# Early-input order in the first microseconds, and stage passages without GpSimd's weight parts

## The chip, the cores and the metric
One core of a Trainium2 chip runs the whole program in one launch. The time is the device time of an execution in microseconds. On this core TensorE (PE) multiplies, VectorE (DVE), ScalarE (ACT) and GpSimd (POOL) do the element-wise work, and SyncE (SP) and ScalarE issue the DMA transfers.

## The reference
Two transformer-like blocks over 256 latent tokens of width 1024, in float32. The first has two layers; in each, 256 context tokens `hc` go along with the latent `h`, and both are modulated by a vector worked out from `c`:

```python
m = (silu(c) @ w_ada + b_ada)                      # 9 x 1024 per layer
h  = post(h,  swiglu(pre(h,  m, 0, 0),  ffn_wi[0], ffn_wo[0]), m, 0, 1, 0.5)
hc = post(hc, swiglu(pre(hc, mc, 0, 0), ffn_wi[0], ffn_wo[0]), mc, 0, 1, 0.5)
...                                                # attention of context and latent, w_o
h = post(h, swiglu(pre(h, m, 6, 4), ffn_wi[1], ffn_wo[1]), m, 6, 5, 0.5)
```

`pre` is an RMS norm with gain and shift, `post` adds the normed and gated result to the residual. The last layer ends with the latent alone. The second block runs over the 256 tokens: a mixer of two scans, a feed-forward product with a short convolution, a gated linear attention, a second feed-forward product; each is `x + norm(f(norm(x)))`.

## The kernel before
**Weights.** All weight matrices are one stream of 128x128 tiles in the order of use, eight to a block of 512 KB. `Weights._dma` loads a block into `raw` (three buffers) by SyncE's queue. `Weights._split` makes two parts of it, `hi`, the block rounded to the matmul's reduced float format (ScalarE, L115), and `lo = raw - hi` (VectorE, L116). A product is then three matmuls, hi by hi, hi by lo, lo by hi (`mm3`, `mm3t`). Where `aside` is above zero, the low part is GpSimd's (L116 on POOL); where `alone` holds too, GpSimd makes the high part as well, as an addition of zero (L113). In the first mixer (`share = 3`) every third low part is GpSimd's. `place` says in which buffers a block's parts go, if not in the three standing pairs. `take` hands out tiles and splits two blocks ahead (`LOOK`), unless the stream is `held`; `to(b)` splits up to block b at once, and `go_on` releases the hold.

**Order.** A scheduler puts each engine's instructions in order by priority and the code's order; each engine then runs its list strictly in that order. `high_priority` moves instructions forward in the list.

**The head.** `run` issues the loads of the vectors (`vec`), the inputs (`hl`, `hc`) and constants on ScalarE's queue; `ada_loads` issues on SyncE's queue the modulation weights of eight chunks (`adaw`, four transfers of 256 KB per chunk), with the first weight blocks between. `pre` squares and norms the four row tiles (`rms_rows`, `hn`), transposes chunk by chunk (`tr`), scales by the modulation (`ux`, ScalarE) and splits the result into `uh` and `ul` (VectorE). `ada_pe` works the modulation of chunk c out: matmuls `adp`, copy `adsb`, transposes `adt`, a reduction, `mod`, `Am`. `group` runs the first products `gp` over the eight chunks with five accumulators (`NG0`).

**The passages.** The program is: feed-forward, attention, feed-forward, feed-forward (512 columns, latent and context together), attention, feed-forward (256 columns), mixer, feed-forward, mixer, feed-forward. A 256-column stage ends with `out_main` and `out_tail`: the product `po` of the last matrix, 16 last products for two row tiles; then per tile a square on ScalarE, `bi`, `yg` and `y` (times the gain), the reciprocal `rs`, the residual `hl` in two halves, the square `jv` on VectorE, and `hn` for the next stage's transposes. The next stage's first blocks are split here too, so that its first products find them. In the 512-column stages `go_on(2)` gives two low parts to GpSimd; `aj` is VectorE's modulation work of later layers.

## Time and profile before

| | us |
|---|---|
| median of 3 runs | 2624.83 (2623.13 to 2625.05) |
| the profiled execution, its own time | 2620.6 |
| its span | 2618.7 |
| TensorE busy | 2532.6 |
| VectorE busy | 1748.1 |
| ScalarE busy | 1156.1 |
| GpSimd busy | 203.9 |

The span is the profiled execution from its first to its last instruction. A busy TensorE is one that has a matmul under way, at whatever clock was granted. The profile names instructions by line, engine, and the tiles written and read (`out<-in`); a number in square brackets behind an instruction is the engine's idle time ahead of it, and what ended that.

### The profile page before, as it was taken

The numbers are of one execution on the slowest core, as the hardware profiler recorded it, in microseconds if no ns is written. First come the engines' busy times: TensorE is split into PE (matmuls) and PEld (weight loads), VectorE is DVE, ScalarE is ACT, GpSimd is POOL, SyncE is SP. The second block draws the span as 40 slices with busy tenths as digits, with TensorE's granted clock in tenths as the row PEclk, the third lists the DMA queues.
The fourth block names the chain that finished last, engine by engine and source line by source line (L and its number), as shares of the span: only waits on it lengthen the run. The fifth ranks groups of instructions, "written<-read, shape, count | busy, mean of one in ns | idle before, by whom it ended". The sixth has DMA issues, their size and how long they took to land.

```text
span 2618.7 us, 37016 instructions
## 1 busy us (share of the span) xinstructions
PE 2532.6 (97%) x13876; PEld 2137.4 (82%) x13876; DVE 1748.1 (67%) x3538; ACT 1156.1 (44%) x1994; POOL 203.9 (8%) x129
## 2 busy tenths in 40 slices
PE   6999999999999999999999999999999899999998
PEld 3888888888888887888888887987977799776997
DVE  4899535565899324998325666557767787666884
ACT  2322224455422223322224555446556565565663
POOL 2000000000000000000000101002352200121000
PEclk9999999999999999999999999999999999999999
DMA  6566331212366222565222313554433355534454
GB/s 254 182 219 216 123 120 63 82 53 73 134 220 214 92 97 97 178 220 189 97 89 87 111 69 136 184 189 150 150 125 128 120 178 186 171 111 137 153 182 157
DMA packets 124741, 375.53 MB, mean 143 GB/s; under 512 B 13840, under 2 KB 15504, under 8 KB 124304
## 3 DMA queue, kind: packets, MB, share of 16 engines
q1 hardware_dynamic: 123408, 369.22, 41.1%
q10 hardware_dynamic: 1152, 3.94, 0.4%
q8 instruction: 109, 1.79, 0.3%
q14 instruction: 72, 0.59, 0.1%
HBM read 372.05 MB, written 1.05 MB: 142 GB/s over the span
## 4 chain that ended last, share of the span: by engine, by line
PE 88%; DVE 6%; ACT 3%; issue 1%; DMA 1%; POOL 1%; SPq 0%; DVEq 0%; ACTq 0%; POOLq 0%
PE pj L172 15%; PE pj L173 15%; PE pj L174 15%; PE po L179 8%; PE po L181 8%; PE po L180 8%; PE pv L708 2%; PE tm L180 1%; PE tm L179 1%; PE tm L181 1%; DVE w L116 1%; PE gp L173 1%; PE gp L172 1%; PE gp L174 1%; ACT w L115 1%
## 5 line engine op out<-in xcount | busy, mean ns | idle before, releaser
L115 ACT ACTIVATE w<-raw 128x1024 fp32r<-128x1024 f32 (+1 forms) x564 | 572.5, 1022 | 984.5 <-PE pj L173 341.4
L116 DVE TENSOR_TENSOR w<-raw,w 128x1024 fp32r<-128x1024 f32 (+1 forms) x533 | 627.5, 1184 | 476.5 <-ACT w L115 468.8
L172 PE MATMUL pj<-uh,w 128*128 128x256 f32 (+1 forms) x2376 | 798.5, 336 | 2.4 <-ACT P L190 2.4
L174 PE MATMUL pj<-uh,w 128*128 128x256 f32 (+1 forms) x2376 | 795.0, 335 | 0.0
L173 PE MATMUL pj<-ul,w 128*128 128x256 f32 (+1 forms) x2376 | 794.6, 334 | 0.0
L172 PEld LDWEIGHTS pj<-uh,w 128*128 128x128 f32 x2376 | 451.9, 190 | 51.6 <-ACT P L190 2.8
L174 PEld LDWEIGHTS pj<-uh,w 128*128 128x128 f32 x2376 | 452.0, 190 | 48.5 <-issue 0.3
L173 PEld LDWEIGHTS pj<-ul,w 128*128 128x128 f32 x2376 | 452.1, 190 | 47.1
L597 DVE SCALAR_TENSOR_TENSOR aj<-adaw,cB 128x512 f32<-128x512 f32 x512 | 360.4, 704 | 9.0 <-DMA adaw<-in_wada 0.2
L179 PE MATMUL po<-w,sh 128*128 128x512 f32 x792 | 312.7, 395 | 0.0
L181 PE MATMUL po<-w,sl 128*128 128x512 f32 x792 | 311.9, 394 | 0.0
L180 PE MATMUL po<-w,sh 128*128 128x512 f32 x792 | 311.2, 393 | 0.0
L181 PEld LDWEIGHTS po<-w,sl 128*128 128x128 f32 x792 | 149.0, 188 | 33.9
L179 PEld LDWEIGHTS po<-w,sh 128*128 128x128 f32 x792 | 148.9, 188 | 33.8 <-DVE yg L193 0.6
L180 PEld LDWEIGHTS po<-w,sh 128*128 128x128 f32 x792 | 148.9, 188 | 33.2 <-DVE w L116 0.3
L116 POOL TENSOR_TENSOR w<-raw,w 128x1024 fp32r<-128x1024 f32 (+1 forms) x46 | 111.7, 2428 | 799.8 <-ACT w L115 784.3
L179 PE MATMUL tm<-w,uh 128*128 128x512 f32 x224 | 90.7, 407 | 0.0
L180 PE MATMUL tm<-w,uh 128*128 128x512 f32 x224 | 88.9, 397 | 0.7 <-POOL w L116 0.5
L193 DVE TENSOR_TENSOR sg<-sg,pj 128x512 f32<-128x512 f32 (+1 forms) x82 | 50.8, 619 | 58.0 <-PE pj L174 57.7
L181 PE MATMUL tm<-w,ul 128*128 128x512 f32 x224 | 88.7, 396 | 0.0
L190 ACT ACTIVATE ux<-tr,mod,Am 128x256 f32<-128x256 f32 (+1 forms) x96 | 49.8, 545 | 71.0 <-PE tr L327 26.4
L327 PE MATMUL tr<-cst,hn 128*128 128x128 f32 x240 | 51.5, 298 | 27.9 <-DVE hn L203 25.7
(340 smaller groups left out, 3139.6 us busy)
## 6 DMA issues: line engine op xcount, KB each, us to landing
raw<-in_w SPq DMA_DIRECT2D x554, 512.0 KB, 3.3
adaw<-in_wada SPq DMA_DIRECT2D x288, 256.0 KB, 3.1
bt<-in_bias SPq DMA_DIRECT2D x12, 192.0 KB, 2.4
hl<-in_x ACTq DMA_DIRECT2D x1, 1024.0 KB, 8.6
hc<-in_x ACTq DMA_DIRECT2D x1, 1024.0 KB, 8.4
gc<-in_gcst ACTq DMA_DIRECT2D x1, 512.0 KB, 3.4
out<-hl SPq DMA_DIRECT2D x2, 256.0 KB, 2.2
out<-hl ACTq DMA_DIRECT2D x2, 256.0 KB, 2.3
```

The lines of the kernel that those rows point to most:

```text
L115: nc.scalar.activation(out=hi, in_=ri, func=ACTF.Copy)
L116: eng.tensor_tensor(out=lo, in0=ri, in1=hi.bitcast(F32), op=ALU.subtract)
L172: mm(ps, w[0], x[0], start=first, stop=False)
L173: mm(ps, w[0], x[1], start=False, stop=False)
L174: mm(ps, w[1], x[0], start=False, stop=last)
L179: mm(ps, x[0], w[0], start=first, stop=False)
L180: mm(ps, x[0], w[1], start=False, stop=False)
L181: mm(ps, x[1], w[0], start=False, stop=last)
L193: self.nc.vector.tensor_tensor(out=out, in0=a, in1=b, op=op)
L327: nc.tensor.transpose(p[:, t * 128:(t + 1) * 128], hn[t][c // 4][:, (c % 4) * 128:(c % 4 + 1) * 128], self.ident)
L597: nc.vector.scalar_tensor_tensor(out=x, in0=w, scalar=1.0, in1=self.cB[:, s, i * 512:(i + 1) * 512], op0=ALU.mult, op1=ALU.mult, accum_out ...
L708: nc.tensor.matmul(po[:, a * 64:a * 64 + 64], x[:, kt * 128:(kt + 1) * 128], vt[k0 + kt][:, vc + a * 64:vc + a * 64 + 64], start=kt == 0, ...
```

## The change
1. In the head, `vec`, the second half of `hl` and the second half of `hc` are issued on SyncE's queue, the first halves on ScalarE's. Two one-element activations load ScalarE's tables for Silu and for the square root ahead of their first use. The first three blocks' parts are no longer GpSimd's. `after_norms` ties the parts of the first five blocks, by order edges within an engine's list, behind the last square and the last `hn`, then behind the `ux` and `ul` of chunks; `ada_pe` of chunk c is tied behind the products `gp` of chunk c-2.
2. In the passages, GpSimd makes no parts: `aside` is no longer set, and `go_on(2)` is `go_on(0)`. The 23 low parts that `share` gives it in the first mixer stay. All others go to ScalarE and VectorE.
3. `out_main` splits up to six blocks ahead and one past the product's end, in place of four and the end. The list of extra places is used twice in a product of more than 16 blocks (feed-forward), so that the parts can be made that early. A place is set for the block three past the end.
4. The pool `up` waits by tile (`reuse_waits="tile"`): a new tile there waits for the users of its own bytes alone.

The products on TensorE are the same, in number and shape. GpSimd loses 21 whole and 2 half low parts and its 15 high parts; ScalarE gets 9 whole and 10 half high parts and two one-element activations more, VectorE 17 whole and 10 half low parts. The rest of the difference is that halves and wholes change places. The diff, cut to what matters:

```diff
             while self.dma_at <= b:
                 self._dma()
             r = self.raws.pop(b)
-            with self.B.tc.high_priority() if urgent and b >= self.B.EARLY else nullcontext():
+            with self.B.tc.high_priority() if urgent and b >= self.B.EARLY else self.B.after_norms():
                 aside = self.aside > 0
                 eng = nc.gpsimd if aside or self.share and b % self.share == 0 else nc.vector
                 self.aside = max(0, self.aside - 1)
...
         self.nc.vector.reciprocal(t, t)
         return t
 
+    @contextmanager
+    def after_norms(self):
+
+        with ExitStack() as es:
+            for x in self.behind[(0, 2, 3, 4, 6)[self.W.split_at]] if self.W.split_at < self.EARLY else ():
+                es.enter_context(self.tc.issue_after(x.ins))
+            yield
+
     def preload(self, func, dep):
 
...
         else:
-            self.sq(h[:, 512:1024], ss[1])
+            self.behind[0][0] = self.sq(h[:, 512:1024], ss[1])
         return self.rstd(ss[1], 1024.0, [128, 1], bias=b)
 
     def normed(self, pool, t):
...
                     for i in range(2):
-                        self.ts(hn[t][i], h[:, i * 512:(i + 1) * 512], r, None, ALU.mult)
+                        self.behind[0][1] = self.ts(hn[t][i], h[:, i * 512:(i + 1) * 512], r, None, ALU.mult)
             for c in range(8):
-                if c == 2 and T == 512:
-                    self.W.go_on(2)
+                if T == 512 and (c == 2 if self.W.pos > NG0 * 8 else c == 7):
+                    self.W.go_on(0)
                 if need is not None:
                     need(c)
                 if c not in us:
...
                         else:
-                            self.act(x[:, o], p[:, o], ACTF.Identity, scale=A(c, t // 2), bias=shift(c, t // 2))
+                            g = self.act(x[:, o], p[:, o], ACTF.Identity, scale=A(c, t // 2), bias=shift(c, t // 2))
                     o = slice(t0 * 128, (t0 + by) * 128)
                     if shift is not None:
                         self.cp(us[c][0][:, o], x[:, o])
-                        self.tt(us[c][1][:, o], x[:, o], us[c][0][:, o].bitcast(F32), ALU.subtract)
+                        v = self.tt(us[c][1][:, o], x[:, o], us[c][0][:, o].bitcast(F32), ALU.subtract)
+                        self.behind.append([g, v])
                 yield us[c], o
 
     def pre1(self, pool, l, k, T, by=None, need=None):
...
 
+
         end = self.W.pos // TPB + n
-        self.W.place.update(zip(range(end - len(places), end), places))
+        m = len(places)
+        self.W.place.update(zip(range(end - m, end), places))
+        if n > 16:
+            self.W.place.update(zip(range(end - 2 * m - 3, end - m - 3), places))
+        if self.up is not None:
+            self.W.place[end + 3] = self.fourth()
         for k in range(n - 4):
             for i in range(2):
                 w = self.W.take(4)
                 if i == 0 and not self.W.held:
-                    self.W.to(min(self.W.pos // TPB + self.LOOK + 2, end))
+                    self.W.to(min(self.W.pos // TPB + 6, end + 1))
                 for t in range(2):
                     if (t, i) not in po:
                         po[t, i] = self.psum("po")
@@ -438,16 +453,10 @@
 
         yg, ss = {}, {}
         g = self.gain_rows([lambda c, i=i: G(i * 4 + c, 0) for i in range(2)])
-        self.W.held = self.W.alone = True
+        self.W.held = True
         ws = [[self.W.take(4) for i in range(2)] for _ in range(4)]
         b = self.W.pos // TPB + 3
-        self.W.to(b - 1)
-        self.W.aside = 1
-        self.W.to(b)
-        if self.up is not None:
-            self.W.place[b] = self.fourth()
-            self.W.aside = 1
-            self.W.to(b + 1)
+        self.W.to(b + 1 if b in self.W.place else b)
         for t in range(2):
             if before is not None:
                 before(t)
...
             c = m % 8
             if m == 8:
-                self.W.go_on(2)
+                self.W.go_on(0)
             if m < 8:
                 if halves:
                     self.W.held = True
                 u.append(x)
                 ws.append([self.W.take() for _ in range(n)])
-            for p, w in zip(ps, ws[c]):
-                self.mm3(p[:, o], w, (x[0][:, o], x[1][:, o]), c == 0, c == 7)
+            for i, (p, w) in enumerate(zip(ps, ws[c])):
+                g = self.mm3(p[:, o], w, (x[0][:, o], x[1][:, o]), c == 0, c == 7)
+                if self.ada_at < 8 and (m == 0 and i == 0 or i == n - 1):
+                    self.ada_behind.append(g)
         return ps, u
 
     def group256(self, us, place):
 
         b = self.W.pos // TPB
-        self.W.held = self.W.alone = True
+        self.W.held = True
         if self.W.split_at <= b + 3:
...
             m = self.mod[l][:, j:j + dj + 1:dj, :]
             two = lambda name, i, d: self.v(name, i, d + 1)[:, ::d].unsqueeze(2).to_broadcast([128, 2, 2])
             if self.ada_at < 8:
-                with self.tc.high_priority() if self.ada_at not in (1, 2) else nullcontext():
+                g = self.ada_behind[self.ada_at - 1:self.ada_at] if self.ada_at else ()
+                with ExitStack() as es:
+                    es.enter_context(self.tc.high_priority())
+                    for x in g:
+                        es.enter_context(self.tc.issue_after(x.ins))
                     self.ada_pe(m)
             else:
                 self.ada_dve(m)
...
             self.vec = const.tile([128, NVEC], F32, name="vec")
             self.cst = const.tile([128, NCST], F32, name="cst")
-            nc.scalar.dma_start(out=self.vec, in_=A["vec"])
-            nc.scalar.dma_start(out=self.hl, in_=A["x"][:, 0:2])
+            nc.sync.dma_start(out=self.vec, in_=A["vec"])
+            nc.scalar.dma_start(out=self.hl[:, 0], in_=A["x"][:, 0])
             nc.scalar.dma_start(out=self.cst, in_=A["cst"])
+            nc.sync.dma_start(out=self.hl[:, 1], in_=A["x"][:, 1])
             self.ident = self.cst[:, 0:128]
             self.blk = self.cst[:, 128:130]
             self.eps = const.tile([128, 1], F32, name="eps")
             nc.vector.memset(self.eps, 1e-6)
+            self.preload(ACTF.Silu, self.eps)
             self.zero = const.tile([128, 1], F32, name="zero")
             nc.vector.memset(self.zero, 0.0)
             self.av = const.tile([128, 32], F32, name="av")
...
                 b1 = e1.enter_context(tc.tile_pool(name="b1", bufs=1))
                 self.hc = b1.tile([128, 2, 1024], F32, name="hc")
-                nc.scalar.dma_start(out=self.hc, in_=A["x"][:, 2:4])
+                nc.scalar.dma_start(out=self.hc[:, 0], in_=A["x"][:, 2])
+                nc.sync.dma_start(out=self.hc[:, 1], in_=A["x"][:, 3])
...
                 self.act(self.cT[:, :, 0:2], cv, ACTF.Silu)
+                self.preload(ACTF.Sqrt, self.cT[:, 0, 0:1])
                 self.cB = b1.tile([128, 2, 1024], F32, name="cB")
                 self.ac = b1.tile([128, NACST], F32, name="ac")
                 self.ada_at = 0
+                self.ada_behind = []
                 self.p1 = e1.enter_context(tc.tile_pool(name="p1", bufs=54))
                 self.adp = e1.enter_context(tc.tile_pool(name="adp", bufs=1))
                 self.ada_loads()
-                self.W.aside, self.W.alone = 2, True
                 self.ffn1(0, 0, 512, 32, NG0, lambda c: self.ada_to(c + 1), (0, 1))
                 self.attn(0, False, 0, (0, 2))
                 self.ffn1(0, 1, 512, 52, nxt=(1, 0))
                 self.ffn1(1, 0, 512, 72, nxt=(1, 1))
                 self.attn(1, True, 72)
                 self.ffn1(1, 1, 256, 72, 4)
-            self.up = ent(name="up", bufs=16)
+            self.up = ent(name="up", bufs=16, reuse_waits="tile")
             self.W.share = 3
             self.by_act = True
             self.mixer0()
```

On ScalarE at the head, between the squares of `hc` and the scaled chunks (`jk` is a square, `rs` the root, `ux` the scaled chunk, `w` a high part of a block), before:

```order
L190 ACTIVATE jk,ss<-hc 128x512 x2
L190 ACTIVATE rs<-ss,bi 128x1
L190 ACTIVATE jk,ss<-hc 128x512 x2
L190 ACTIVATE rs<-ss,bi 128x1
L190 ACTIVATE ux<-tr,mod_91,Am_93 128x256 x12
L115 ACTIVATE w<-raw 128x1024
L190 ACTIVATE ux<-tr,mod_91,Am_93 128x256 x4
```
and now:

```order
L191 ACTIVATE jk,ss<-hc 128x512 x2
L191 ACTIVATE rs<-ss,bi 128x1
L191 ACTIVATE jk,ss<-hc 128x512 x2
L115 ACTIVATE w<-raw 128x1024
L191 ACTIVATE rs<-ss,bi 128x1
L191 ACTIVATE ux<-tr,mod_95,Am_97 128x256 x4
L115 ACTIVATE w<-raw 128x1024
L191 ACTIVATE ux<-tr,mod_95,Am_97 128x256 x2
```
The first block's high part stands ahead of the last tile's root, and the next ones between the chunks.

On VectorE at the end of the attention of the second layer, ahead of the 256-column feed-forward product (`w` is a low part, `G` the gain, `bi` to `hl` the first row tile's residual), before:

```order
L116 TENSOR_TENSOR w<-raw,w 128x512 x6
L208 COPY G<-gr 128x512
L116 TENSOR_TENSOR w<-raw,w 128x512 x2
L116 TENSOR_TENSOR w<-raw,w 128x1024
L205 TENSOR_SCALAR bi<-ss 128x1
L193 TENSOR_TENSOR yg<-po,G 128x512
L116 TENSOR_TENSOR w<-raw,w 128x1024
L193 TENSOR_TENSOR y_13898<-po,G 128x512
L241 RECIPROCAL rs<-rs 128x1
L199 SCALAR_TENSOR_TENSOR hl<-yg,rs,hl 128x512
```
and now:

```order
L116 TENSOR_TENSOR w<-raw,w 128x512 x6
L209 COPY G<-gr 128x512
L116 TENSOR_TENSOR w<-raw,w 128x512 x2
L116 TENSOR_TENSOR w<-raw,w 128x1024 x3
L116 TENSOR_TENSOR w<-raw,w 128x512 x2
L206 TENSOR_SCALAR bi<-ss 128x1
L194 TENSOR_TENSOR yg<-po,G 128x512
L194 TENSOR_TENSOR y_13914<-po,G 128x512
L242 RECIPROCAL rs<-rs 128x1
L200 SCALAR_TENSOR_TENSOR hl<-yg,rs,hl 128x512
```
The whole low part that stood behind `yg` has moved ahead of `bi`, and one more whole and two halves with it.

On VectorE at the end of the second mixer, ahead of the last feed-forward product (`oo` and `mxl` are the mixer's output and its low part), before:

```order
L199 SCALAR_TENSOR_TENSOR oo<-oo,rs,sr 128x256 x4
L116 TENSOR_TENSOR w<-raw,w 128x1024 x2
L199 SCALAR_TENSOR_TENSOR mxl<-tf,vec,mxh 128x256 x3
L116 TENSOR_TENSOR w<-raw,w 128x1024 x2
L199 SCALAR_TENSOR_TENSOR mxl<-tf,vec,mxh 128x256
L205 TENSOR_SCALAR bi<-ss 128x1
L193 TENSOR_TENSOR yg<-po,G 128x512
L193 TENSOR_TENSOR y_22450<-po,G 128x512
L241 RECIPROCAL rs<-rs 128x1
L199 SCALAR_TENSOR_TENSOR hl<-yg,rs,hl 128x512
```
and now:

```order
L200 SCALAR_TENSOR_TENSOR oo<-oo,rs,sr 128x256 x4
L116 TENSOR_TENSOR w<-raw,w 128x1024 x2
L200 SCALAR_TENSOR_TENSOR mxl<-tf,vec,mxh 128x256 x3
L116 TENSOR_TENSOR w<-raw,w 128x1024 x2
L200 SCALAR_TENSOR_TENSOR mxl<-tf,vec,mxh 128x256
L116 TENSOR_TENSOR w<-raw,w 128x1024
L206 TENSOR_SCALAR bi<-ss 128x1
L194 TENSOR_TENSOR yg<-po,G 128x512
L116 TENSOR_TENSOR w<-raw,w 128x1024
L194 TENSOR_TENSOR y_22472<-po,G 128x512
L242 RECIPROCAL rs<-rs 128x1
L200 SCALAR_TENSOR_TENSOR hl<-yg,rs,hl 128x512
```
Two more low parts: one ahead of `bi`, one between `yg` and `y`.

## Rows read from the trace of the kernel before

**Rows 1.** Page, part 1, TensorE to GpSimd: busy time, share, instructions.
```profile
PE 2532.6 (97%) x13876; PEld 2137.4 (82%) x13876; DVE 1748.1 (67%) x3538; ACT 1156.1 (44%) x1994; POOL 203.9 (8%) x129
```

**Rows 2.** Waits of TensorE: engine, line waited for; us in all, times, longest.
```profile
PE tr L327 <- DVE hn L203: 25.7, 11, 4.7
```

**Rows 3.** Timeline, TensorE, head: start, duration, instruction; first weight matmul.
```profile
33.46 0.49 PE L172 MATMUL gp<-uh,w 128*128 128x512 f32 x1
```

**Rows 4.** Windows: length, busy times, clock (PEclk), DMA share, GB/s; head, two passages.
```profile
24.00:33.46 9.46, 3.94 (x24) 2.11 (x24) 6.81 (x15) 3.63 (x10) 4.15 (x2) 0.52 1.04 397
1794.30:1801.20 6.90, 4.49 (x12) 3.41 (x13) 5.69 (x11) 3.61 (x14) 4.64 (x4) 0.51 0.13 39
2268.80:2275.60 6.80, 4.21 (x12) 3.00 (x13) 6.76 (x13) 2.79 (x9) 4.09 (x2) 0.50 0.45 153
```

**Rows 5.** Timeline, GpSimd, head: first and last of six.
```profile
15.03 1.94 POOL L113 TENSOR_TENSOR w<-raw,zero 128x1024 fp32r<-128x1024 f32 x1 [14.58 <-DMA raw<-in_w]
...
25.83 2.40 POOL L116 TENSOR_TENSOR w<-raw,w 128x1024 fp32r<-128x1024 f32 x1
```

**Rows 6.** Timeline, VectorE, head: two `hn` pairs beside GpSimd, one after.
```profile
19.51 4.49 DVE L203 TENSOR_SCALAR hn<-hl,rs 128x512 f32<-128x512 f32 x2
...
24.68 3.83 DVE L203 TENSOR_SCALAR hn<-hc,rs 128x512 f32<-128x512 f32 x2
...
29.20 0.88 DVE L203 TENSOR_SCALAR hn<-hc,rs 128x512 f32<-128x512 f32 x2
```

**Rows 7.** Timeline, TensorE, passages: first instruction after each long wait.
```profile
684.88 0.71 PE L172 MATMUL gp<-uh,w 128*128 128x256 f32 x2 [1.72 <-DVE uh L208]
...
1064.28 0.50 PE L172 MATMUL gp<-uh,w 128*128 128x256 f32 x2 [1.65 <-DVE uh L208]
...
1596.77 1.82 PE L327 MATMUL tr<-cst,hn 128*128 128x128 f32 x5 [4.73 <-DVE hn L203]
...
1796.71 0.80 PE L179 MATMUL gp<-w,uh 128*128 128x512 f32 x1 [2.76 <-ACT uh L190]
...
2070.02 0.50 PE L181 MATMUL po<-w,mxl 128*128 128x512 f32 x1 [2.94 <-DVE bi L205]
...
2270.81 0.90 PE L327 MATMUL tr<-cst,hn 128*128 128x128 f32 x3 [4.24 <-DVE hn L203]
...
2419.51 0.87 PE L327 MATMUL tr<-cst,hn 128*128 128x128 f32 x3 [3.63 <-DVE hn L203]
```

**Rows 8.** Timeline, VectorE, passages: beside GpSimd and alone.
```profile
681.88 2.73 DVE L597 SCALAR_TENSOR_TENSOR aj<-adaw,cB 128x512 f32<-128x512 f32 x1
...
685.87 0.68 DVE L597 SCALAR_TENSOR_TENSOR aj<-adaw,cB 128x512 f32<-128x512 f32 x1
...
1590.91 2.86 DVE L199 SCALAR_TENSOR_TENSOR hl<-y,rs,hl 128x512 f32<-128x512 f32 x1
...
1795.51 0.75 DVE L199 SCALAR_TENSOR_TENSOR hl<-yg,rs,hl 128x512 f32<-128x512 f32 x1
...
2269.56 3.70 DVE L203 TENSOR_SCALAR hn<-hl,rs 128x512 f32<-128x512 f32 x2
```

**Rows 9.** Page, part 5: parts of a block, busy us, mean ns | idle, releaser.
```profile
L115 ACT ACTIVATE w<-raw 128x1024 fp32r<-128x1024 f32 (+1 forms) x564 | 572.5, 1022 | 984.5 <-PE pj L173 341.4
L116 DVE TENSOR_TENSOR w<-raw,w 128x1024 fp32r<-128x1024 f32 (+1 forms) x533 | 627.5, 1184 | 476.5 <-ACT w L115 468.8
```

**Rows 10.** Timeline, ScalarE, head: first square, root's table, first scaled chunk.
```profile
9.85 0.63 ACT L190 ACTIVATE jk<-hl 128x512 f32<-128x512 f32 x1 [2.17 <-DMA hl<-in_x]
...
11.34 1.28 ACT L190 ACT_TABLE_LOAD   x1
...
30.25 1.02 ACT L190 ACTIVATE ux<-tr,mod,Am 128x256 f32<-128x256 f32 x2 [1.28 <-PE tr L327]
```

**Rows 11.** DMA issues, 0 to 42 us and page: size, median us to landing.
```profile
raw<-in_w SPq DMA_DIRECT2D x6, 512.0 KB, 6.4
...
raw<-in_w SPq DMA_DIRECT2D x554, 512.0 KB, 3.3
```

17 lines of the change are left out of this document (8 added, 9 removed).

## The prediction
> **What bounds the kernel now.** I read the page first: TensorE is busy 2532.6 us of the 2618.7 us span, 97% [rows 1]. The 86 us that are left are what this change can reach, plus what TensorE works at half clock. The reader is to see next, in the table of who waited for whom, that the largest single item is the transposes waiting for VectorE's `hn`, 25.7 us in 11 waits [rows 2]; everything else is spread thinly. Two kinds of place hold these waits. The first is the head: the first matmul with a weight starts at 33.46 us [rows 3]; in the stretch 24 to 33.46 us the granted clock is 0.52 [rows 4], the lower of its two levels (1.2 of 2.4 GHz), after TensorE had stood idle. There the DMA engines are saturated (share 1.04, 397 GB/s), but VectorE has a second burden: GpSimd splits the first three blocks between 15.03 and 28.2 us, six instructions of 1.9 to 2.4 us of which the first and the last are shown [rows 5], and in that time an `hn` pair takes 4.49 and 3.83 us on VectorE, against 0.88 us just after [rows 6]. The second kind is the passages, where one product ends and the next stage's norm must be ready: TensorE waits 4.73, 2.76, 2.94, 4.24 and 3.63 us at the five passages with 256 columns and 1.72 and 1.65 us at two of the 512-column ones [rows 7]. In each, GpSimd is splitting a weight block while VectorE does the residual and norm; `hl`, which takes 0.75 us alone, takes 2.86, and an `hn` pair 3.70 [rows 8].
>
> **The head.** The change takes the six GpSimd instructions away and gives the parts to ScalarE (1.02 us for a high part) and VectorE (1.18 us for a low part) [rows 9], in an order in which they stand behind the norms and between the chunks' own steps. It also splits the two input transfers in halves over two queues, which lets the first square begin before 9.85 us, where ScalarE waited for the whole `hl`, and loads the square root's table earlier than at 11.34 us, where 1.28 us of loading lay in the chain [rows 10]. What is late next: ScalarE's four pairs of squares are 1.5 us each, from 9.85 to 11.34 for the first [rows 10], so 6 us from about 8; then the first block, which has landed at 15.03 when GpSimd begins on it [rows 5]. About 4.2 MB stand ahead of its end in the new queue order against 4.7 MB before (counted from the issues), and at 397 GB/s [rows 4] that is 1.3 us less, so it lands at 13.7 to 15. High part 1.02, the last root and `hn` some 1.2, transposes 0.5, `ux` 1.02 (the pair at 30.25) [rows 10], `uh` 0.4 by estimate: the first weight matmul stands near 18 us, with 16.5 and 21 as ends. That is 15.5 us earlier. From it I take 1.2 us (modulation and transposes of the next two chunks, which TensorE had done while it waited and must now do between products) and 2 us (the first products at half clock; the stretches of half clock at the passages are up to 6.9 us long [rows 4], so 0 to 3.4). **Head: 12 us, 8 to 15.** The transfers don't take it back as I reckon it: a chunk needs 1.05 MB of modulation weights and 5/8 of a 0.5 MB block, 1.38 MB, 3.5 us at 397 GB/s, against an estimated 4 us of TensorE per chunk (15 products, four transposes, the modulation's own matmuls).
>
> **The two 512-column passages.** At 681.88 an `aj` took 2.73 us beside GpSimd instead of 0.68, and `uh` and TensorE waited behind it [rows 7, 8]. Undoing that gives 2.05; but the low part now stands on VectorE itself, 1.18 us. 0.9 us each, and at 684.9 up to 1.7 us of half clock. **2.5 us, 1 to 4.**
>
> **The five 256-column passages.** Here the same trade is made five times: a stretch goes, a queue of parts comes. VectorE and ScalarE do their work in the order of the program, so a part that stands ahead of `bi` holds back the whole norm.
> At 1596.77 three whole and two half low parts stand ahead of `bi`, where one whole stood there and one behind `yg`: two and a half to three more, 3.0 to 3.6 us. The stretches that go are at least the 2.1 us of the one `hl` [rows 8] and at most the 4.73 us of the wait [rows 7]: -1.5 to +1.7, I take 0, since the parts wait for transfers too.
> At 1796.71 the wait is 2.76; the parts are done before the tail, and a high part, 1.02 us, now stands ahead of `uh`: 1.5 us, with 1 and 4.5 as ends, the upper if the half clock (6.9 us at 0.51 [rows 4]) goes too.
> At 2070.02 the wait is 2.94; two low parts, 2.4 us, come between `yg` and the reciprocal, partly in time in which VectorE waited for ScalarE anyhow: 1.5 us, 0.5 to 2.9.
> At 2270.81 the wait is 4.24. The `hn` pair alone loses 2.8 us to GpSimd [rows 6, 8]. All 22 low parts stand ahead of `bi` now, where 19 stood and one more behind `yg`; whether they are done in time depends on how far the transfers have run ahead. 3 us, 1 to 6 with the half clock of 6.8 us [rows 4].
> At 2419.51 the wait is 3.63; one low part, 1.18 us, comes ahead of `bi`, and one ahead of `y` in time in which VectorE waits for ScalarE: 2.5 us, 1 to 5.
> **Sum: 8.5 us, 2 to 19.**
>
> What the rows show of the stretch: the `hn` pair of 24.68 ends at 28.51 [rows 6], right after GpSimd's last part at 28.23 [rows 5]; it is held until GpSimd is done, not slowed in proportion. That is how the Trainium skill has it in "SBUF — State Buffer", section "Who interferes with whom": VectorE's second port pair is GpSimd's only one, and whoever comes second is blocked until the other's instruction ends. By that rule alone, with nothing counted for the new queue, the whole of the waits of rows 7 would go (21.7 us in place of my 11, which would make it 2591 us). The page says nothing of the 1.2 us that each part now takes on VectorE itself, and for that reason I stay with the sum by rows.
>
> **The rest** is nothing: the same products run on TensorE, the 23 low parts that GpSimd has in the first mixer stay where they are, and both feed-forward products leave VectorE idle enough for the parts that come sooner. If that cover failed, each low part would cost its 1.18 us.
>
> **Sum:** 12 + 2.5 + 8.5 = 23 us. The profiled execution took 2620.6 us around its 2618.7 us span, so 2597.6; the median of the runs is 2624.83, 0.16% above it, so I put the changed kernel at 2602 us. All low ends give 11 us less (2614), all high ends 38 us less (2587).
>
> **Rivals.**
> 1. *The queue takes the place of the stretch.* At every passage the added parts wait for their transfers and `bi` stands behind them, as I reckon it for 1596.77. A block takes 3.3 us to land [rows 11], 1.02 and 1.18 us to split, 5.5 us for a buffer, of which there are three: three more blocks are 5.5 us, against a mean wait of 3.66 us, the rest hidden by the tail. Then only the head stays: 2613, between 2609 and 2618. For it: the order. Against it: the parts may start six blocks ahead.
> 2. *The head is held by its transfers.* The DMA engines were saturated all the way [rows 4], and the landing order decides. If the pace of a chunk is the transfers', and the first matmul starts at 21 with TensorE waiting in each chunk, the head gives 4 us and the sum is 15: 2610.
> 3. *Slower.* At the ends of the 22-block products VectorE must finish three more blocks before `bi`. If a block takes 6.4 us to land, as the first six did [rows 11], in place of 3.3, a buffer's turn is 8.6 us, and so are three blocks: less the 3.66 us of wait that go, 5 us are lost at each of five passages, 25 in all, against 14.5 won at the head and the 512-column passages: 2635. It decides from a landing time of about 5 us on: then the loss of the passages reaches what the head gives. Against it: the engines are half idle there.
> 4. *The change doesn't do what it says*, the first products still wait for something at 30 us (the order edges are queue order only): 2625, within 4.
>
> **How the numbers follow.** Forecast 0.68, rival 1 0.14, rival 2 0.08, rival 3 0.05, rival 4 0.05. A measurement of this kernel can tell about 0.2% from no change, 5.2 us: faster means under 2619.6. The forecast, rival 2 and nearly all of rival 1 are faster, 0.87; rival 4 and the edge of rival 1 are within, 0.08; rival 3 is slower, 0.05. The range 2590 to 2618 takes in the forecast, rivals 1 and 2, without the outermost end of the sum.
>
> **What would show it.** In the changed profile: the first weight matmul at 16.5 to 21 us; no GpSimd split before the first mixer; `hl` at 0.75 and the `hn` pair at 0.88 us in the passages. The sum of TensorE's waits for `hn` falls from 25.7 to under 10 us. If it stays above 15 with undisturbed `hn`, rival 1 holds, and `bi` stands late behind `w`. If TensorE waits for `adaw` or `raw` between 18 and 45 us, rival 2 holds. The prediction is wrong if parts of a later block, on ScalarE or VectorE, stand in front of a step that TensorE waits for at a place where it didn't wait before.

## The result

The changed kernel takes 2593.23 us (median, 2590.59 to 2594.48) against 2623.98 us (2621.81 to 2625.05) for the one before: a ratio of 0.9883, with a 95% interval of 0.9865 to 0.9900, 30.8 us less. The forecast was 2602, the range 2590 to 2618. The profiled execution fell from 2620.6 to 2590.59 us, its span from 2618.7 to 2588.8.

The page of the changed kernel, its busy line (against [rows 1]) and TensorE's waits for `hn` (against [rows 2]):

```profile
PE 2523.4 (97%) x13876; PEld 2132.9 (82%) x13876; DVE 1733.9 (67%) x3565; ACT 1169.8 (45%) x2015; POOL 117.6 (5%) x91
```
```profile
PE tr L336 <- DVE hn L204: 10.6, 6, 6.2
```

GpSimd fell from 203.9 to 117.6 us, and TensorE's waits for `hn` from 25.7 to 10.6 (13.1 in a second trace of the changed kernel, e11 below). TensorE's own busy time fell by 9 us at the same instructions, which fits fewer stretches at half clock (shown at single places below).

The first weight matmul and the first instruction after each wait at the 256-column passages, in the timeline of the changed kernel (against [rows 3, 7]; the passages stand 15 to 30 us earlier now):

```profile
21.64 0.79 PE L173 MATMUL gp<-uh,w 128*128 128x512 f32 x1 [1.57 <-DVE uh L209]
22.37 0.79 PE L174 MATMUL gp<-ul,w 128*128 128x512 f32 x1
...
1582.08 1.82 PE L336 MATMUL tr<-cst,hn 128*128 128x128 f32 x5 [6.20 <-DVE hn L204]
...
1777.80 0.50 PE L180 MATMUL gp<-w,uh 128*128 128x512 f32 x1 [2.31 <-ACT uh L191]
...
1779.92 0.48 PE L336 MATMUL tr<-cst,hn 128*128 128x128 f32 x1 [1.38 <-DVE bi L206]
...
2050.95 0.33 PE L973 MATMUL tf<-cst,hm 128*128 128x128 f32 x1 [1.65 <-DVE mxl L200]
...
2248.70 0.55 PE L336 MATMUL tr<-cst,hn 128*128 128x128 f32 x3 [0.64 <-DVE hn L204]
...
2390.94 0.52 PE L336 MATMUL tr<-cst,hn 128*128 128x128 f32 x3 [0.76 <-ACT y L191]
```

The head starts 11.8 us earlier; the passage at 1582 waits *longer*, 6.20 against 4.73. At the next, the kernel before waits twice, and rows 7 show the second wait only (2.76); the first stands in its timeline here:

```profile
1793.17 0.55 PE L327 MATMUL tr<-cst,hn 128*128 128x128 f32 x3 [2.00 <-DVE hn L203]
```

So 2.31 and 1.38 stand in place of 2.00 and 2.76; the third passage has 1.65 in place of 2.94; and at the last two 4.24 and 3.63 have become 0.64 and 0.76.

A ledger needs more than the waits, because of the clock (numbers are rounded). For each product of TensorE I took the start of the same matmul in both traces (the k-th `gp`, `po`, `pj` and so on; the difference is the median of 12 around a time) and noted by how much the changed kernel is ahead; a row is what the lead grows by in its stretch. The second column is a second profiled execution of the changed kernel (run e11 below):

```
stretch (time in the trace of before)      first trace   second trace   forecast
head, to 680 us                               10.9           10.3          12
512-column passage, 680 to 1055                2.6            3.5           } 2.5
512-column passage, 1055 to 1420               3.0            2.1           }
second attention, 1420 to 1560                -0.2            1.3           -
passage at 1597, to 1612                      -0.8           -0.2           0
passage at 1797, to 1812                       1.4            1.7           1.5
first mixer, to 2057                          -0.6           -0.4           -
passage at 2070, to 2085                       2.0            1.8           1.5
passage at 2271, to 2290                       6.2            4.5           3
second mixer, to 2400                          1.4           -0.1           -
passage at 2420, to the end                    3.7            3.5           2.5
sum                                           29.7           28.1          23
```

### The profile page after: what moved, and what is told of

Same layout as the page of the kernel before. It is cut to its first block, busy times and chain, and to the rows that moved or that the text cites. A ratio compares the mean times of both kernels' runs of the same rounds, so it can differ in the third digit from the quotient of the medians.

```text
span 2588.8 us, 37013 instructions
## 1 busy us (share of the span) xinstructions
PE 2523.4 (97%) x13876; PEld 2132.9 (82%) x13876; DVE 1733.9 (67%) x3565; ACT 1169.8 (45%) x2015; POOL 117.6 (5%) x91
## 3 DMA queue, kind: packets, MB, share of 16 engines
HBM read 372.05 MB, written 1.05 MB: 144 GB/s over the span
## 4 chain that ended last, share of the span: by engine, by line
PE 89%; DVE 4%; ACT 3%; DMA 2%; issue 1%; POOL 1%; SPq 0%; DVEq 0%; ACTq 0%; POOLq 0%
PE pj L173 15%; PE pj L174 15%; PE pj L175 15%; PE po L180 8%; PE po L182 8%; PE po L181 8%; PE pv L722 2%; DVE w L116 2%; PE tm L180 2%; PE tm L182 1%; PE tm L181 1%; DMA raw<-in_w 1%; PE gp L173 1%; PE gp L174 1%; PE gp L175 1%; ACT w L115 1%
## 5 line engine op out<-in xcount | busy, mean ns | idle before, releaser
L115 ACT ACTIVATE w<-raw 128x1024 fp32r<-128x1024 f32 (+1 forms) x583 | 587.6, 1016 | 1002.7 <-PE pj L174 349.2
L116 DVE TENSOR_TENSOR w<-raw,w 128x1024 fp32r<-128x1024 f32 (+1 forms) x560 | 655.5, 1178 | 466.5 <-ACT w L115 457.8
L607 DVE SCALAR_TENSOR_TENSOR aj<-adaw,cB 128x512 f32<-128x512 f32 x512 | 352.8, 689 | 8.7
L200 DVE SCALAR_TENSOR_TENSOR cv<-pj,vec,cv 128x255 f32<-128x255 f32 x160 | 75.7, 479 | 2.4
L174 PE MATMUL gp<-ul,w 128*128 128x256 f32 (+1 forms) x232 | 70.6, 308 | 0.8 <-DVE ul L194 0.8
```

Source lines behind the costliest of these rows:

```text
L115: nc.scalar.activation(out=hi, in_=ri, func=ACTF.Copy)
L116: eng.tensor_tensor(out=lo, in0=ri, in1=hi.bitcast(F32), op=ALU.subtract)
L174: mm(ps, w[0], x[1], start=False, stop=False)
L200: self.nc.vector.scalar_tensor_tensor(out=out, in0=a, scalar=s, in1=b, op0=op0, op1=op1)
L607: nc.vector.scalar_tensor_tensor(out=x, in0=w, scalar=1.0, in1=self.cB[:, s, i * 512:(i + 1) * 512], op0=ALU.mult, op1=ALU.mult, accum_out ...
```

## The experiments

Two theories stood against each other. **Held:** GpSimd's instructions hold VectorE's norms and residuals up, and to have them gone is the gain. **Early:** the deeper look-ahead, the places and the order of the inputs make things ready sooner, and GpSimd is beside the point. All differences "to the changed kernel" are taken between medians; that of the changed kernel is 2593.2 in the first comparison and 2591.8 when it ran again (e11). The eight runs of the changed kernel lie between 2588.9 and 2594.5 us, and an interval of one ratio is some 4 us wide to each side. So a difference of 4 or 5 us rests on the single runs: all of e1, e2, e5, e6 and e7 lie above those eight, and three of e8's four; those of e3, e4 and e9 overlap with them. The edits shown are against the changed kernel, cut where `...` stands.

**e1, the head alone.** The kernel before with the head of the change; the passages, look-ahead and places as before.

```diff
...
-                    self.W.to(min(self.W.pos // TPB + 6, end + 1))
+                    self.W.to(min(self.W.pos // TPB + 4, end))
...
-        self.W.to(b + 1 if b in self.W.place else b)
+        self.W.to(b - 1)
+        self.W.aside = 1
+        self.W.to(b)
...
-                self.W.go_on(0)
+                self.W.go_on(2)
...
```

> The kernel before with the head of the change alone (input halves on two queues, table preloads, first blocks' parts on ScalarE and VectorE behind the norms); all passages as before, with GpSimd's parts and the shallow look-ahead. Between the two traces the program stands 11.0 us earlier at 680 us, when the head is over, and 29.7 us at the end. Theory: head and passages add up, so this kernel is 11 us faster than the one before (10 to 12) and 19 slower than the changed one; first weight matmul at 21.6 us. Rival: the head's gain is partly the passages' doing (less VectorE work late, other clock), and less than 7 us are left of it.

Measured: 2611.62 us, ratio 0.9952 (0.9937 to 0.9967), 12.3 us faster than before, 18.4 slower than the changed kernel. Head and passages add up, as the ledger says. In its trace the lead is 10.4 us when the head is over and 8.9 at the end: the wait at the passage of 2271 is 5.90 us in this execution, against 4.24 before.

**e2, GpSimd back in the 256-column tails**, everything else as changed.

```diff
-        self.W.to(b + 1 if b in self.W.place else b)
+        self.W.alone = True
+        self.W.to(b - 1)
+        self.W.aside = 1
+        self.W.to(b)
+        if b in self.W.place:
+            self.W.aside = 1
+            self.W.to(b + 1)
+        self.W.aside, self.W.alone = 0, False
```

> The changed kernel, with one or two blocks' parts given back to GpSimd in the tail of each 256-column stage; look-ahead, places and head as changed. Theory (GpSimd's instructions hold VectorE's residual and norm up): 6 to 12 us slower than the changed kernel, with hl, jv and hn of 1.5 to 3.7 us again in the tails. Rival (the look-ahead makes the parts early enough, GpSimd's absence is not what counts): within 3 us of the changed kernel.

Measured: 2603.78 us, ratio 0.9921 (0.9905 to 0.9938), 10.6 us slower than the changed kernel. In the timeline of e2, the tail at 2250 us (GpSimd, VectorE, TensorE):

```profile
2246.75 5.17 POOL L116 TENSOR_TENSOR w<-raw,w 128x1024 fp32r<-128x1024 f32 x2
...
2247.00 2.68 DVE L200 SCALAR_TENSOR_TENSOR hl<-yg,rs,hl 128x512 f32<-128x512 f32 x1
2249.61 2.86 DVE L200 SCALAR_TENSOR_TENSOR hl<-y,rs,hl 128x512 f32<-128x512 f32 x1
...
2254.57 0.55 PE L336 MATMUL tr<-cst,hn 128*128 128x128 f32 x3 [3.91 <-DVE hn L204]
```

In the changed kernel the same `hl` takes 0.75 us:

```profile
2245.18 0.75 DVE L200 SCALAR_TENSOR_TENSOR hl<-yg,rs,hl 128x512 f32<-128x512 f32 x1
```

The two `hl` end at 2249.68 and 2252.47, each some 0.5 us after one of GpSimd's two instructions (single records: 2249.14 and 2251.91), and the wait is back at 3.91. With the look-ahead in place, GpSimd's parts still cost 10.6 us by the medians, of the 11.3 to 12.5 that the ledger has for these passages. *Held* stands; *early* alone falls.

**e6, GpSimd busy with nothing.** Is it that GpSimd is busy, or that its parts come late? Here it adds a tile to itself beside the norms; nobody reads the result.

```diff
         h = self.ht(t)
+        if self.up is not None and t == 0 and not self.last:
+            for x in range(4):
+                d = self.tmp.tile([128, 512], mybir.dt.bfloat16, tag="dmy", bufs=1, name="dmy")
+                self.gt(d, yg[t, 0], yg[t, 0], ALU.add)
```

> The changed kernel, with four additions on GpSimd put in the first row tile's tail of the three passages of the second block (512 columns each, two inputs from the state buffer, started when yg is written); nothing reads what they write. Theory (any GpSimd instruction that reads the state buffer holds VectorE's two-input instructions until it ends): hl of 1.2 us and more in place of 0.75, and the whole 3 to 9 us slower than the changed kernel. Rival (before, it was the late parts of a block, not GpSimd's being busy, that cost the time): less than 1 us slower.

Measured: 2600.2 us, ratio 0.9903 (0.9886 to 0.9919), 7.0 us slower than the changed kernel. In the timeline of e6:

```profile
2247.57 5.38 POOL L197 TENSOR_TENSOR dmy<-yg 128x512 bf16<-128x512 f32 x4 [192.10 <-ACT rs L191]
...
2248.11 1.05 DVE L200 SCALAR_TENSOR_TENSOR hl<-yg,rs,hl 128x512 f32<-128x512 f32 x1
2249.08 1.52 DVE L200 SCALAR_TENSOR_TENSOR hl<-y,rs,hl 128x512 f32<-128x512 f32 x1
2250.64 1.41 DVE L280 SCALAR_TENSOR_TENSOR jv<-hl 128x512 f32<-128x512 f32 x1
...
2253.43 0.73 PE L336 MATMUL tr<-cst,hn 128*128 128x128 f32 x3 [4.14 <-DVE hn L204]
```

GpSimd's four additions take 5.38 us together, and `hl`, `hl` and `jv` go from 0.75, 0.75 and 0.69 to 1.05, 1.52 and 1.41 us, 1.8 us in all: each ends some 0.5 us after one of the first three additions (single records: 2248.61, 2250.06 and 2251.50). TensorE waits 4.14 us in place of 0.64, and not all of that is the hold: the last low part ahead of `bi` waited for its transfer, and `bi` came at 2246.66, 2.9 us later than in the changed kernel's first trace, where the whole program stands 1.2 us later. In the second trace, too, the wait is 2.25 us (last section), and 4.14 is 1.9 above that. The passage at 2400 is cleaner: `hl` and `jv` lose 1.5 us there, and TensorE waits 2.46 us in place of 0.76 and 0.95. Nobody reads what the additions write, so what holds VectorE is GpSimd's being busy. That is the exclusive lock of the Trainium skill ("SBUF — State Buffer", "Who interferes with whom"), which names VectorE's instructions with two inputs from the state buffer; `hl` and `jv` are such.

**e7, the shallow look-ahead**, GpSimd still out.

```diff
-        m = len(places)
-        self.W.place.update(zip(range(end - m, end), places))
-        if n > 16:
-            self.W.place.update(zip(range(end - 2 * m - 3, end - m - 3), places))
+        self.W.place.update(zip(range(end - len(places), end), places))
...
-                    self.W.to(min(self.W.pos // TPB + 6, end + 1))
+                    self.W.to(min(self.W.pos // TPB + 4, end))
```

> The changed kernel with the look-ahead of out_main as before (four blocks, the product's end as limit) and the extra places used once. Theory (the gain is GpSimd's absence): within 2.5 us of the changed kernel. Rival (without the deeper look-ahead the parts queue ahead of bi, as they do in the second attention's tail): at the tails after the feed-forward products TensorE waits 2 to 4 us again and the whole is 4 to 10 us slower.

Measured: 2597.47 us, ratio 0.9897 (0.9882 to 0.9912), 4.2 us slower than the changed kernel: more than *held* expected, and at the low end of what its rival did. In the timeline of e7, VectorE and TensorE in the tail at 2250:

```profile
2242.76 0.15 DVE L206 TENSOR_SCALAR bi<-ss 128x1 f32<-128x1 f32 x1
...
2246.45 1.23 DVE L116 TENSOR_TENSOR w<-raw,w 128x1024 fp32r<-128x1024 f32 x1 [1.28 <-ACT w L115]
...
2248.37 1.22 DVE L116 TENSOR_TENSOR w<-raw,w 128x1024 fp32r<-128x1024 f32 x1
...
2249.71 0.75 DVE L200 SCALAR_TENSOR_TENSOR hl<-yg,rs,hl 128x512 f32<-128x512 f32 x1
...
2253.23 0.55 PE L336 MATMUL tr<-cst,hn 128*128 128x128 f32 x3 [3.24 <-DVE hn L204]
```

Three low parts (the last two are shown) stand between `bi` and `hl`, the second of them waiting 1.28 us for its high part, and `hl` begins at 2249.71, 4.5 us later than in the changed kernel, where the whole program stands 1.7 us later; TensorE waits 3.24 us. Both theories have a share, then: at this passage the lead over the kernel before grows by 1.9 us with the shallow look-ahead, by 6.2 and 4.5 with the deep one. Taking GpSimd out pays in full only if the parts that VectorE takes over are done before `bi`, and the look-ahead does that. At the passage of 2400 the shallow kernel waits 0.91 where the changed one waits 0.76: there GpSimd's absence is enough.

**e8, GpSimd back in the 512-column passages.**

```diff
-                    self.W.go_on(0)
+                    self.W.go_on(2 if self.W.pos > NG0 * 8 else 0)
...
-                self.W.go_on(0)
+                self.W.go_on(2)
```

> The changed kernel, with two low parts per 512-column passage given back to GpSimd as before. Between the traces of before and after, the program gains 2.6 us around 685 us and 3.0 around 1065. Theory (aj, uh and ul are held by GpSimd there): 4 to 6.5 us slower than the changed kernel, aj of 2.7 us and waits of 1.7 us for uh again. Rival (the low part on VectorE costs nearly what the stretch did, as the prediction's sum has it): 1 to 3 us slower.

Measured: 2597.73 us, ratio 0.9894 (0.9880 to 0.9909), 4.5 us slower than the changed kernel, with one of the four runs at 2592.5. In the timeline of e8, GpSimd and TensorE at the second of them:

```profile
1048.91 2.79 POOL L116 TENSOR_TENSOR w<-raw,w 128x1024 fp32r<-128x1024 f32 x1 [368.83 <-ACT w L115]
...
1052.52 0.51 PE L173 MATMUL gp<-uh,w 128*128 128x256 f32 x2 [1.75 <-DVE uh L209]
```

and in that of the changed kernel VectorE at the first, where TensorE has no wait above 0.3 us:

```profile
670.73 1.22 DVE L116 TENSOR_TENSOR w<-raw,w 128x1024 fp32r<-128x1024 f32 x1
671.87 0.49 DVE L209 CAST uh<-ux 128x256 fp32r<-128x256 f32 x2
```

The low part (`w`, 1.22 us) is there, and `uh` waits behind it, but TensorE still has products of the stage before.

**e5, GpSimd back in the head** for the first two blocks (the kernel before gave it three by 28.2 us), with inputs, preloads and order as changed.

```diff
...
+                self.W.aside, self.W.alone = 2, True
                 self.ffn1(0, 0, 512, 32, NG0, lambda c: self.ada_to(c + 1), (0, 1))
```

> The changed kernel, with the first two blocks' parts given back to GpSimd; the order of the inputs, the table preloads and the order edges stay. Theory (in the head too it is GpSimd's instructions that hold VectorE's norms up): an hn pair of 2 to 4.5 us again, the first weight matmul at 25 to 30 us in place of 21.6, and the whole 4 to 8 us slower than the changed kernel. Rival (the split inputs and the preloads give the head's gain): first weight matmul before 23, less than 2 us slower.

Measured: 2598.35 us, ratio 0.9901 (0.9887 to 0.9916), 5.1 us slower than the changed kernel. In its timeline:

```profile
14.98 4.39 DVE L204 TENSOR_SCALAR hn<-hl,rs 128x512 f32<-128x512 f32 x2
...
16.68 2.40 POOL L116 TENSOR_TENSOR w<-raw,w 128x1024 fp32r<-128x1024 f32 x1
...
27.91 0.77 PE L173 MATMUL gp<-uh,w 128*128 128x512 f32 x1 [1.67 <-DVE uh L209]
```

An `hn` pair takes 4.39 us, until 0.3 us after GpSimd's second instruction ends, and the first weight matmul stands at 27.91: 6.3 of the 11.8 us. The other 5.5 (33.46 to 27.91) are GpSimd's third block, the order, the split inputs and the preloads together; I didn't separate them.

**e3, the copy in the way.** In the changed kernel VectorE stands still at 10.9 us, although the squares of the second tile are done. Its timeline (VectorE, TensorE):

```profile
10.72 0.14 DVE L206 TENSOR_SCALAR bi<-ss 128x1 f32<-128x1 f32 x1
14.29 0.42 DVE L209 COPY adsb<-adp 128x256 f32<-128x256 f32 x1 [3.42 <-PE adp L576]
...
14.82 0.88 DVE L204 TENSOR_SCALAR hn<-hl,rs 128x512 f32<-128x512 f32 x2
...
11.23 3.01 PE L576 MATMUL adp<-adaw,cT 128*32 128x256 f32 x16 [11.23 <-DMA adaw<-in_wada]
```

`adsb`, the copy of the first chunk's modulation, stands ahead of the second tile's reciprocal; its matmuls wait for the last weights until 11.23 and take 3.01 us, where the sixteen of the next chunk (at 23.52) take 1.94 and those of a later one (at 29.95) 1.07. TensorE had done nothing before; why they are so slow, no run shows, since no trace has a record of the clock as early as this (last section).

```diff
...
-        self.cp(sb[:, :256], p[:, :256])
+        with self.tc.issue_after(self.hns[2].ins) if self.ada_at == 0 else nullcontext():
+            self.cp(sb[:, :256], p[:, :256])
```

> The changed kernel, with the copy adsb of the first modulation chunk tied behind the third row tile's hn on VectorE. In the changed kernel VectorE stands from 10.9 to 14.29 us waiting for that chunk's matmuls, with the second tile's reciprocal and hn queued behind. Theory (that queue is what sets the first weight matmul at 21.64): it starts at 18 to 19 us, and the whole is 2.5 to 3.5 us faster than the changed kernel. Rival (the first block's landing and its parts, or the modulation, set it as well): less than 1 us faster.

Measured: 2590.51 us, ratio 0.9872 (0.9857 to 0.9887), 2.7 us less than the changed kernel's median, whose interval overlaps. The traces show a gain, but not its size: from 25 to 600 us the products stand 1.7 to 2.0 us earlier than in the first trace of the changed kernel, and from 30 us on only 0.7 to 0.9 earlier than in the second, where TensorE's clock rose 2 us sooner (25.4 against 27.4 us). In the timeline of e3:

```profile
16.57 1.22 DVE L116 TENSOR_TENSOR w<-raw,w 128x1024 fp32r<-128x1024 f32 x1
...
17.90 0.23 DVE L207 TENSOR_SCALAR Am<-mod,vec 128x2 f32<-128x2 f32 x1
...
19.76 0.80 PE L174 MATMUL gp<-uh,w 128*128 128x512 f32 x1 [3.19 <-DVE uh L210]
```

The first weight matmul is at 19.76, not at 18 to 19: now the first low part, 1.22 us, stands ahead of `mod` and `Am`.

**e4, a shorter queue in the second attention's tail.** In the changed kernel (ScalarE, VectorE):

```profile
1574.54 1.16 ACT L115 ACTIVATE w<-raw 128x512 fp32r<-128x512 f32 x2 [1.60 <-DMA raw<-in_w]
1575.60 0.57 ACT L191 ACTIVATE yg<-po 128x512 f32<-128x512 f32 x1
...
1575.20 1.29 DVE L116 TENSOR_TENSOR w<-raw,w 128x512 fp32r<-128x512 f32 x2 [1.01 <-ACT w L115]
1576.42 0.15 DVE L206 TENSOR_SCALAR bi<-ss 128x1 f32<-128x1 f32 x1
```

The square `yg` waits behind a high part that waits 1.60 us for its transfer, and `bi` behind the low part.

```diff
-        self.W.to(b + 1 if b in self.W.place else b)
+        self.W.to(b - 1 if self.up is None else b + 1 if b in self.W.place else b)
...
-            self.W.place[self.W.pos // TPB + len(oh) + 3] = self.halves()
```

The condition holds in the tail of the next feed-forward product, too, which loses one block; TensorE's two waits there stay as they were (2.30 and 1.38 us).

> The changed kernel, with two blocks fewer split in the tail of the second attention (they follow in the next stage, behind the first tile's residual). There TensorE waits 6.20 us for hn in the changed kernel, 4.73 in the one before. Theory (the low parts ahead of bi wait for their transfers, and the norm behind them): the wait falls to 1.5 to 3.5 us and the whole is 3 to 4.5 us faster than the changed kernel. Rival (the products of the next stage then wait for these parts): the wait moves to gp and less than 1 us is won.

Measured: 2589.13 us, ratio 0.9868 (0.9853 to 0.9882), 4.1 us less than the changed kernel, and 2.7 less than when that ran again. In its timeline:

```profile
1578.11 0.52 PE L336 MATMUL tr<-cst,hn 128*128 128x128 f32 x3 [2.13 <-DVE hn L204]
...
1582.22 0.80 PE L180 MATMUL gp<-w,uh 128*128 128x512 f32 x1 [1.62 <-DVE bi L206]
```

The wait falls from 6.20 to 2.13, and 1.62 come back at `gp`, where two parts now stand ahead of `bi` and `uh` of the second tile: 2.0 us net against the first trace of the changed kernel, 1.3 against the second. That the queue made the wait is shown by the wait; that the whole gains the 3 to 4.5 us expected is not.

**e9, the pool's waits as before.**

```diff
-            self.up = ent(name="up", bufs=16, reuse_waits="tile")
+            self.up = ent(name="up", bufs=16)
```

> The changed kernel without the tile-wise waits of the pool up (as before, a new tile waits for the users of what stood in its place as a whole). Theory (those waits matter only at the entry of the first mixer, where before uh waited 2.76 us): 1 to 3 us slower than the changed kernel, at 1780 us. Rival (they count at every entry into a pool, in the feed-forward products too): 5 us slower or more. Neither: no difference beyond 1 us.

Measured: 2590.99 us, ratio 0.9873 (0.9858 to 0.9888): 2.2 us below the changed kernel's first median and 0.8 below its second, no difference that these runs can show. Neither theory holds, and part 4 of the change is worth nothing that can be measured here. TensorE waits once for 3.75 us instead of twice for 2.31 and 1.38:

```profile
1776.99 0.77 PE L180 MATMUL gp<-w,uh 128*128 128x512 f32 x1 [3.75 <-ACT uh L191]
```

**e10, both queues shortened**, with the edits of e3 and e4, the first low part behind the first `Am`, and the second of the two blocks split at the third chunk.

```diff
...
-                    eng.tensor_tensor(out=lo, in0=ri, in1=hi.bitcast(F32), op=ALU.subtract)
+                    with self.B.tc.issue_after(self.B.am0.ins) if b == 0 else nullcontext():
+                        eng.tensor_tensor(out=lo, in0=ri, in1=hi.bitcast(F32), op=ALU.subtract)
...
             if m == 0:
+                self.W.to(b + 3)
+            if m == 2:
                 self.W.to(b + 4)
...
```

> The changed kernel with three edits: the first chunk's adsb behind the third hn; the first block's low part behind the first Am; in the second attention's tail two blocks fewer, of which one is split at the third chunk of the next stage. Theory (the two queues found are independent): first weight matmul at 18.3 to 19 us, wait for hn at 1580 us about 2 us, and the whole 4.5 to 7 us faster than the changed kernel, 2586 to 2589. Rival (what is won early is lost where TensorE meets the next wait, or to its clock): within 2 us of the changed kernel.

Measured: 2586.36 us, ratio 0.9853 (0.9837 to 0.9869), 6.9 us less than the changed kernel, as the theory had it; the first weight matmul came at 19.06, just behind its 19. In its timeline:

```profile
19.06 0.80 PE L176 MATMUL gp<-uh,w 128*128 128x512 f32 x1 [2.18 <-DVE uh L212]
...
1575.39 0.52 PE L340 MATMUL tr<-cst,hn 128*128 128x128 f32 x3 [1.95 <-DVE hn L207]
```

**e11 and e12, the changed and the combined kernel side by side** on one chip.

> The changed kernel itself, on the same chip and against the same runs of before as the next one. Theory: 2591 to 2595 us. Its half-clock stretches of the second block (none between 2240 and 2290 us in its first trace) need not stand where they stood: if they are chance, this trace has one there and its span is about 2 us longer.

> The combined kernel (adsb behind the third hn, the first low part behind Am, two blocks fewer in the second attention's tail) again, beside the changed kernel. Theory (4.1 us in the tail, 2.5 in the head): 5 to 8 us below the changed kernel on the same chip. Rival (the difference between the two medians was the chip's): less than 2 us.

Measured: 2591.8 us for the changed kernel, ratio 0.9875 (0.9857 to 0.9892), and 2583.73 for the combined one, ratio 0.9847 (0.9832 to 0.9863): 8.1 us apart, just above the 5 to 8 expected. The two intervals still overlap by a little, but the combined kernel came out 6.9 and 8.1 us lower in the two comparisons, and the traces show 2.5 us of it in the head and some 3 to 4 at the second attention. The other 2 us come behind 2085 us, where two executions of one program differ by as much (last section); no edit accounts for them.

## Why the prediction was right, and where not

**The mechanism** was the one forecast: GpSimd holding VectorE. e2, e5, e6 and e8 show it at each kind of place. Of the signs that were named, `hl` at 0.75 and the `hn` pair at 0.88 us came, and no GpSimd split stands before the first mixer (the first is at 1793.2). Two were missed: the first weight matmul, at 21.64 in place of 21 at the latest, and the waits for `hn`, at 10.6 and 13.1 in place of under 10. The sign of being wrong came at one step: at 1779.92 TensorE waits 1.38 us for a `bi` that stands behind a low part, and before it had no wait over 0.5 us there. The passage gained even so.

**The head**, forecast 12 us (8 to 15), gave 10.3 to 10.9. Its steps were less good than their sum: two errors went opposite ways, and that they nearly cancelled is luck. I put the first weight matmul at 18, with 21 as the late end; it came at 21.64. The step that failed is the list of what is late next: it had ScalarE's squares and the first block's landing, and not that `adsb` queues ahead of the second tile's norm on VectorE, though the order of before has it there too; in e3 and e10 the first weight matmul stands 1.9 and 2.6 us earlier. On the other side I deducted 3.2 us that were not lost: from the first weight matmul to the first `pj` the kernel before took 45.6 us (33.46 to 79.1), the changed one 45.9. The slow first products were paid for (21.64 and 22.37, 0.73 us apart, where later ones follow each other in 0.23), but TensorE has no idle time in that stretch any more, where before it had 1.3 us (45.64 us less 44.31 busy).

**The 512-column passages**, forecast 2.5 us (1 to 4), gave 5.6 in each trace, and undoing them cost 4.5 by the medians (e8). The term was mis-sized by one deduction: I took 1.18 us off each for the low part's own time on VectorE. That time lies where TensorE still has products, so it costs nothing there; and the half clock at 685 us went with the wait.

**The 256-column passages**, forecast 8.5 us (2 to 19), gave 12.5 in the first trace and 11.3 in the second. One by one: 1597 was put at 0 (-1.5 to +1.7) and gave -0.8 and -0.2, by the mechanism that was named: parts that wait for transfers, in front of `bi`; e4 shows it by shortening the queue. 1797 and 2070, 1.5 each, gave 1.4 to 1.7 and 1.8 to 2.0. At 1797 that is luck: the forecast priced the wait of 2.76 for ScalarE's `uh`, with `hl` at 0.75 us alone, and this fell only to 2.31; what went is the wait of 2.00 for `hn`, which it hadn't listed and which had the held `hl` of that passage (2.89 us, at 1788.18) ahead of it; and 1.38 came anew. 2271, put at 3, gave 6.2 and 4.5; 2420, put at 2.5, gave 3.7 and 3.5. In the last two I was too careful: at 2271 the 22 parts were done nearly in time, which hung on the look-ahead (e7) and on the transfers (below), and at 2420 only 0.76 and 0.95 us are left of the wait of 3.63.

**"By the rule alone"**, with every wait of [rows 7] gone, would have been 2591, and the measured time is nearer to that than to my sum: the passages gave 18.1 and 16.9 us by the two traces, of 21.7 (23.7 with the wait of 2.00 at 1793.17). What is missing is the new queue, with 6.20 us of waiting at 1582 and 3.7 at 1778. What makes up for part of it is the half clock that goes with a wait: at 685 us 3.5 us were won with a wait of 1.72 (the lead goes from 10.9 to 14.4, and 0.9 of it is gone again by 1055). The rule says nothing of either.

**Rival 1**, the queue in place of the stretch, is true of one passage of five, and would have been true of a second without the look-ahead. **Rival 2** fell: TensorE has no wait for a weight between 21.64 and 67 us, although the transfers run at 395 GB/s until the first matmul and at 335 from there to 46 us (length, busy times of TensorE, its weight loads, VectorE, ScalarE and GpSimd, granted clock, DMA share, GB/s):

```profile
11.00:21.64 10.64, 5.07 (x22) 1.82 (x22) 5.71 (x18) 5.47 (x15) 0.00 (x0) 1.00 1.04 395
21.64:46.00 24.36, 24.36 (x148) 15.95 (x148) 11.17 (x27) 6.92 (x11) 0.00 (x0) 1.00 0.91 335
46.00:67.58 21.58, 21.58 (x143) 15.74 (x143) 12.81 (x28) 10.15 (x15) 0.00 (x0) 1.00 0.27 98
```

**Rivals 3 and 4** fell with the result. Rival 3's own terms would have let it decide from a landing time of 4.4 us on, not 5: 14.5 us over five passages is 2.9, plus the mean wait of 3.66, less 2.2 for the two parts. "The rest is nothing" came out about so: in the first mixer, where 23 parts stayed with GpSimd, the lead shrank by 0.4 to 0.6 us, and in the second attention and the second mixer it changed by -0.2 to 1.4.

## What to carry to other kernels

Work given to an idle engine isn't free when that engine shares a port with the one that is on the path: look at the durations of the busy engine's instructions beside it, not at its share. When the work goes back to the busy engine, look at what it queues in front of; a part that waits for a transfer holds all that is behind it, and whether that costs anything is decided by how far ahead the transfers run. A gap closed is worth more than its length if TensorE's clock fell after it. And before a difference of 2 us between two traces is put down to an edit, look at a second trace of the same program.

## What was not expected of the hardware

The record of the granted clock starts late. In the first trace of the changed kernel the column reads 1.00 from 11 to 21.64 us and on to 46 us (the windows above), while `adp` and the first `gp` run at less than half their later pace. But that trace has its first record of the clock at 27.4 us, and a stretch without a record is printed as 1.00. The second trace of the same program, e11, has its first record at 15.1 us, and from 18.50 to 25.40 it shows half clock (columns as in the windows above):

```profile
18.50:25.40 6.90, 4.19 (x20) 1.56 (x20) 3.30 (x6) 1.38 (x4) 0.00 (x0) 0.51 1.05 391
```

Its first `gp` start at 21.68, 22.41 and 23.00, as slowly after each other as in the first trace, and from 25.42 on at the later pace. So the first products do run at the lower level, as the prediction's deduction had it, though 0.59 to 0.73 us apart is more than twice the later 0.23, so the clock isn't all of it; of `adp` at 11.23, ahead of every record, the traces don't show it.

The passage at 2249 us is paced by transfers, not by what TensorE has won. The second trace, e11, stands 1.8 us ahead of the first there, and yet `bi` comes at nearly the same moment, since the last parts wait for their blocks. First trace, then second (ScalarE, VectorE, and TensorE for the second):

```profile
2241.49 1.07 ACT L115 ACTIVATE w<-raw 128x1024 fp32r<-128x1024 f32 x1 [0.88 <-DMA raw<-in_w]
...
2243.73 0.15 DVE L206 TENSOR_SCALAR bi<-ss 128x1 f32<-128x1 f32 x1
```
```profile
2241.33 1.06 ACT L115 ACTIVATE w<-raw 128x1024 fp32r<-128x1024 f32 x1 [1.26 <-DMA raw<-in_w]
...
2243.57 0.15 DVE L206 TENSOR_SCALAR bi<-ss 128x1 f32<-128x1 f32 x1
...
2248.54 0.55 PE L336 MATMUL tr<-cst,hn 128*128 128x128 f32 x3 [2.25 <-DVE hn L204]
```

The wait is 2.25 us in place of 0.64: the lead is lost here. In seven other runs whose code at this passage is the same (e3, e4, e5, e8, e9, e10, e12) the wait lies between 0.59 and 2.62 us. After it the clock differs too. The windows of the first and the second trace, with the same columns:

```profile
2262.00:2285.00 23.00, 22.83 (x123) 18.29 (x122) 17.98 (x32) 18.25 (x31) 1.62 (x2) 1.00 0.41 137
```
```profile
2262.00:2285.00 23.00, 22.84 (x100) 17.67 (x99) 15.84 (x29) 16.48 (x27) 1.63 (x2) 0.85 0.33 114
```

The first trace has its half clock later (0.51 from 2290.4 to 2297.3 us, where the second reads 1.00). So the row of the ledger at 2271 differs by 1.7 us between two executions of one program, and the medians scatter by some 2 us for reasons that no edit made: e3's trace is longer than that of the changed kernel, 2590.6 against 2588.8, although its head is 1.7 us shorter and its median lower. Why the half clock comes at one execution there and not at the other stays open: e9 waits 0.59 us at this passage and has it, too (0.85 in the same window).
